# Eight very small loads ahead of the last but one store of a strided attention kernel

## Chip, cores and metric

The kernel runs on one core of a Trainium2 chip. The metric is the device time of one execution in microseconds (us); lower is better. Several runs of a kernel are given by their median.

## What is computed

Q, K and V are float32 arrays of 8 x 12 x 1024 x 64 (batch, head, position, depth). Every query attends to the 16 keys at the positions 0, 64, 128, ... of its head:

```python
attend_positions = np.arange(0, seq, stride)          # seq 1024, stride 64
k = K[:, :, attend_positions, :]
v = V[:, :, attend_positions, :]
scores = np.einsum('bhqd,bhkd->bhqk', q, k) * scale
weights = np.exp(scores - np.max(scores, axis=-1, keepdims=True))
weights = weights / (np.sum(weights, axis=-1, keepdims=True) + 1e-10)
result[:, :, i, :] = np.einsum('bhqk,bhkd->bhqd', weights, v)[:, :, 0, :]
```

All of Q is read (25.2 MB) and the whole output is written (25.2 MB); of K and V a sixteenth is read.

## The kernel before

The 96 heads are handled in NG = 24 groups of four. A group of Q is 1 MB and so is a group of the output. The work of a group runs through a pipeline whose steps are written out in the list ORDER: cast to bf16 (POOL, L352), transpose in 32x32 blocks (DVE, L368), scores (PE, L376), largest and subtraction (DVE, L398 and L402), exponential (ACT, L407), sums and reciprocals (DVE, L412 and L416), weights (POOL, L424), transposed weights (PE, L436, copied by ACT in L446), output products (PE, L452) and two copies of the output from PSUM to SBUF (ACT, L470). Q has 11 buffers (`qn`), the output 8 (`out_sb`, in four pairs).

`Program` records every operation with what it reads and writes; `plan` works out which waits are needed, and `emit` issues the operations engine by engine, with PE, DVE and ACT in loops for the middle groups. A transfer has a lane, which is a semaphore that it raises by 16 when it has landed.

All transfers are issued by SP, on one DMA queue, in this order: the rows of K (L288), group 0 of Q (the helper at L34), the rows of V into the tile `v_raw` (L288), groups 1 to 10 of Q, and then what `queue(g)` puts there as group g leaves the pipeline: the load of a later group into a buffer that has come free, and the store of the output. The stores of groups 0 to 15 are of 1 MB each; groups 16 to 21 go in three stores of 2 MB (two groups each); group 22 (`g == NG - 2`) has a store of its own. A store waits until ACT has copied the group (L470). `v_raw` is read by `values(...)` alone, on POOL (L336) and ACT, which spread V into `v_all` in the first microseconds of the kernel.

After the recorded operations SP waits for ACT's last one, a small copy at L579. POOL waits for all lanes whose name begins with `out` and frees the semaphores. SP goes through a few semaphore steps (L185), issues the store of group 23 (`end = send(NG - 1, 1)`, also at L34) and waits for it to land (L617). So the order on SP near the end is: store of groups 20 and 21, store of group 22, wait for ACT, store of group 23, wait for its landing.

Of the kernel before, what the change touches and what calls it, by code (L numbers as in the profile page):

```python
# [18 lines left out]
def _ap_with(ap: bass.AP, new_ap, extra_offset: int = 0) -> bass.AP:  # L19
    return dataclasses.replace(  # L20
        ap, ap=[list(p) for p in new_ap], offset=ap.offset + extra_offset
    )


def _copy(nc, out: bass.AP, in_: bass.AP):

    sides = [
        mybir.BassSymbolicTensorAccessPattern(
            ap=side.ap, dtype=side.dtype, bass_ap=side,
            is_dma=True, for_custom_bir_dma=True,  # L30
        )
        for side in (in_, out)
    ]
    return nc.sync.add_instruction(  # L34
        mybir.InstDMACopy(
            name=nc.get_next_instruction_name(), engine=mybir.EngineType.SP,
            ins=sides[:1], outs=sides[1:], queue="qSPDynamicHW",
            mode="Copy",
        )
    )  # L40


class Program:
# [9 lines left out]
    def op(self, engine, fn, reads=(), writes=(), after=(), lane=None, gate=None, gates=(), times=1, lands=None, last=False):  # L53
        i = len(self.ops)
        deps, own = set(after), set()
        for k in reads:
            deps.add(self.writer.get(k))
            own.add(self.writer.get(k))
        for k in writes:
            deps.update(self.readers.get(k, ()))  # L60
            deps.add(self.writer.get(k))
            own.add(self.writer.get(k))
        deps.discard(None)
        for k in reads:
            self.readers.setdefault(k, []).append(i)
        for k in writes:
            self.writer[k], self.readers[k] = i, []
        first, end, _ = self.loops.get(engine, (0, 0, 1))
        self.ops.append(dict(
            engine=engine, fn=fn, lane=lane or engine, deps=deps, own=own, gate=gate, gates=gates,  # L70
            times=times, lands=lands, last=last, looped=first <= self.turn < end,
        ))
        return i
# [142 lines left out]
def kernel(  # L216
# [8 lines left out]
    nc = tc.nc  # L225

    B, H, S, D = Q.shape
# [5 lines left out]
    NG = B * H // HG  # L233
# [19 lines left out]
    v_raw = sb.tile([P, NC, D], FP32, name="v_raw")  # L253
# [21 lines left out]
    op = prog.op  # L275
    stored = {}

    def load(g):
        n = 32
        op("SP", lambda: _copy(  # L280
            nc, qn[g % QBUFS],
            _ap_with(Q, [[HG * SD // n, n], [1, HG * SD // n]], g * HG * SD),
        ), writes=[f"qn{g % QBUFS}{h}" for h in range(2)], lane=f"q{g % QBUFS}")
# [10 lines left out]
    for g in range(1, QBUFS):  # L294
# [8 lines left out]
       writes=[f"k_t{c}{s}" for c in range(2) for s in range(4)])  # L303
# [183 lines left out]
    def store(g, n):  # L487
        both = range(g, g + n)
        sent = op("SP", lambda: send(g, n), lane=f"out{g % OBUFS}",
                  reads=[f"out{i % OBUFS}.{n}" for i in both for n in range(2)])  # L490
        stored.update((i, sent) for i in both)
# [38 lines left out]
    def queue(g):  # L530
        for n in range(g + QBUFS + ahead if g else QBUFS, g + QBUFS + ahead + 1):
            if n < NG:
                load(n)
        if g < SINGLE or g == NG - 2:
            store(g, 1)
        elif g % RUN == RUN - 1 and g < NG - 1:
            store(g - RUN + 1, RUN)

    def at(i, stage, lag):
# [28 lines left out]
        elif 0 <= g < NG and stage in stages:  # L568
            stages[stage](g)

    stages = dict(sums=sums, largest=largest, raise_=raise_, queue=queue)
    ORDER = "transpose0 turn3 spread3 sums2 cast-1 values2 outA4 largest1 evA4 outB4 evB4 scores0 weights2 raise_1 queue5".split()
    for i in range(2, NG + 5):
# [48 lines left out]
```

## Time and profile before

| | us |
|---|---|
| median of 3 runs | 129.3 (128.73, 129.30, 129.41) |
| the profiled execution | 129.4 |
| its span on the core | 127.6 |

| engine | busy us | share of the span |
|---|---|---|
| ACT | 95.1 | 75% |
| DVE | 86.4 | 68% |
| POOL | 76.5 | 60% |
| PE | 66.0 | 52% |

The span runs from the first to the last instruction of the program on the core; 1.8 us of the execution's time lie outside it. Times in the trace are us from the start of the span. In the rows of stretches each engine has its busy time and its count of instructions, and the last columns are the granted TensorE clock, the mean busy share of the core's 16 DMA engines, and GB/s; a packet counts in the stretch in which it starts, so that a share of a short stretch can be over 1. SPq stands for instructions that issue DMAs on SP, with the time that the issuing took; the time from the start of an issue to the landing of its data is given apart.

### The profile page before, as it was taken

Reading aid. Unit: us, or ns where it says so; the run is one execution under the profiler, and the core shown is the slowest. Engines: PE = TensorE matmul, PEld = TensorE weight load, DVE = VectorE, ACT = ScalarE, POOL = GpSimd, SP = SyncE. Lnnn points to the kernel's source line nnn. Section 1 sums busy time; section 2 is a strip of 40 time slices with the busy share of each in tenths; the row PEclk is TensorE's granted clock in tenths of the full one; section 3 lists DMA queues with packets and bytes.
Section 4 is the critical chain, followed back from the end, with each engine's and each line's share of the span. In section 5 each row is a group of like instructions: output and inputs, shape, how many; then the busy total and the mean of one; then the engine's idle time right before and its main releaser. Section 6 shows DMA issues by size and latency. Waiting matters only on the chain.

```text
span 127.6 us, 2563 instructions
## 1 busy us (share of the span) xinstructions
PE 66.0 (52%) x896; PEld 53.3 (42%) x896; DVE 86.4 (68%) x131; ACT 95.1 (75%) x118; POOL 76.5 (60%) x71
## 2 busy tenths in 40 slices
PE   0000896249666666666666666638446875940000
PEld 0000775148644445555555445426435763720000
DVE  4842597974999999999999999989559360000000
ACT  4259498119999999989999999895693999980000
POOL 2079959999688888888889887573765033000000
PEclk9999999855999999999999999995996899998555
DMA  2999999999979899899899999999899999999960
GB/s 52 408 390 390 483 411 421 462 390 452 442 336 526 339 424 501 357 416 478 377 437 444 401 439 470 385 449 475 357 413 437 419 437 431 426 442 416 401 280 18
DMA packets 7283, 51.15 MB, mean 401 GB/s; under 512 B 3824, under 2 KB 3824, under 8 KB 3824
## 3 DMA queue, kind: packets, MB, share of 16 engines
q1 hardware_dynamic: 7280, 51.12, 95.8%
q14 instruction: 3, 0.02, 0.1%
HBM read 25.95 MB, written 25.17 MB: 401 GB/s over the span
## 4 chain that ended last, share of the span: by engine, by line
DMA 21%; ACT 19%; DVE 16%; issue 6%; POOL 4%; PE 2%; SPq 0%; DVEq 0%; ACTq 0%
DMA qn<-in_Q_dram 21%; ACT out_sb L470 12%; DVE qt L368 6%; ACT wb L446 5%; DVE total L412 3%; DVE top L398 3%; ACT ex L407 2%; DVE low L402 2%; DVE rec L416 2%; PE tp L436 2%; POOL wt_all L424 2%; POOL qb L352 1%; POOL v_all L336 1%; PE o L452 0%; SPq L34 0%
## 5 line engine op out<-in xcount | busy, mean ns | idle before, releaser
L470 ACT COPY out_sb<-o 128x1024 f32<-128x1024 f32 x48 | 46.9, 1043 | 0.0
L352 POOL CAST qb<-qn 128x2048 bf16<-128x2048 f32 (+1 forms) x24 | 42.7, 1783 | 6.6 <-DMA qn<-in_Q_dram 6.4
L368 DVE STREAM_TRANSPOSE qt<-qb 128x1024 int32<-128x1024 int32 x24 | 29.8, 1241 | 9.4 <-POOL qb L352 9.3
L436 PE MATMUL tp<-identity,wt_all 128*128 128x128 bf16 x224 | 19.4, 236 | 31.4 <-POOL wt_all L424 30.1
L424 POOL TENSOR_TENSOR wt_all<-ex,rec 128x512 bf16<-128x512 f32 x24 | 25.4, 1057 | 16.5 <-DVE rec L416 16.3
L452 PE MATMUL o<-v_all,wb 128*128 x224 | 32.9, 294 | 1.4 <-ACT out_sb L470 1.4
L446 ACT COPY wb<-tp 128x1024 bf16<-128x1024 bf16 x25 | 25.6, 1025 | 8.6 <-PE tp L436 8.0
L376 PE MATMUL sc<-k_t,qt 128*128 x448 | 21.6, 201 | 15.4 <-DVE qt L368 14.5
L436 PEld LDWEIGHTS tp<-identity,wt_all 128*128 128x128 bf16 x224 | 14.4, 106 | 33.9 <-POOL wt_all L424 32.5
L376 PEld LDWEIGHTS sc<-k_t,qt 128*128 128x128 bf16 x448 | 18.3, 103 | 21.4 <-issue 20.1
L452 PEld LDWEIGHTS o<-v_all,wb 128*128 128x128 bf16 x224 | 22.3, 106 | 5.4 <-issue 1.3
L407 ACT ACTIVATE ex<-low 128x512 f32<-128x512 f32 x27 | 17.7, 655 | 4.8 <-DVE low L402 4.4
L412 DVE TENSOR_REDUCE total<-ex 128x32 f32<-128x512 f32 x24 | 15.6, 651 | 4.4 <-ACT ex L407 4.4
L402 DVE TENSOR_TENSOR low<-sc,top 128x512 f32<-128x512 f32 x24 | 16.6, 692 | 0.8
L398 DVE TENSOR_REDUCE top<-sc 128x32 f32<-128x512 f32 x24 | 15.2, 632 | 1.3 <-PE sc L376 1.3
L416 DVE RECIPROCAL rec<-total 128x32 f32<-128x32 f32 x24 | 8.5, 353 | 0.8
L309 POOL MEMSET v_all<- 128x4096 bf16 x1 | 3.5, 3511 | 5.2 <-DVE v_all L308 5.2
L336 POOL CAST v_all<-v_raw 32x128 bf16<-32x128 f32 (+1 forms) x12 | 5.1, 428 | 0.6
L322 ACT COPY k_t<-out_sb 32x384 bf16<-32x384 bf16 x8 | 4.1, 508 | 1.8 <-DVE out_sb L313 1.7
L349 ACT CAST qb<-qn 128x1024 bf16<-128x1024 f32 x3 | 3.1, 1040 | 0.0
L336 ACT CAST v_all<-v_raw 32x640 bf16<-32x640 f32 x4 | 2.9, 722 | 0.1
L302 DVE MEMSET k_t<- 128x1792 uint32 x1 | 1.6, 1552 | 1.9 <-issue 1.9
(17 smaller groups left out, 7.7 us busy)
## 6 DMA issues: line engine op xcount, KB each, us to landing
qn<-in_Q_dram SPq DMA_DIRECT2D x24, 1024.0 KB, 17.4
out_dram<-out_sb SPq DMA_DIRECT2D x18, 1024.0 KB, 19.0
out_dram<-out_sb SPq DMA_DIRECT2D x3, 2048.0 KB, 14.9
out_sb<-in_K_dram SPq DMA_DIRECT2D x1, 384.0 KB, 4.2
v_raw<-in_V_dram SPq DMA_DIRECT2D x1, 384.0 KB, 7.1
```

What stands on the lines that cost most here:

```text
L352: op("POOL", lambda: nc.gpsimd.tensor_copy(out=b[:, rows], in_=q[:, rows]), reads=[f"qn{g % QBUFS}{h}" for h in keys] + apart, writes=[f"q ...
L368: op("DVE", lambda *_: nc.vector.transpose(_ap_with(words, [words.ap[0], [1, 2], [D, 16], [2, 32]]), qb[g % 2].bitcast(I32),), reads=[f"qb ...
L376: r = nc.tensor.matmul(sc_ps[g % 2][:, 64 * i : 64 * i + 64], lhsT=_ap_with(qt[g % 2], [qt[g % 2].ap[0], [2, P]], extra_offset=2 * P * i + f),
L398: op("DVE", lambda *_: nc.vector.tensor_reduce(out=m, in_=s, op=ALU.max, axis=mybir.AxisListType.X,), reads=[f"sc{g % 2}"], writes=[f"top{ ...
L402: op("DVE", lambda *_: nc.vector.tensor_tensor(out=low, in0=s, in1=m.unsqueeze(2).to_broadcast([P, 32, NK]), op=ALU.subtract,), reads=[f"s ...
L407: op("ACT", lambda *_: nc.scalar.activation(out=ex[g % 2], in_=low, func=AF.Exp, bias=0.0, scale=scale,), reads=["low"], writes=[f"ex{g % ...
L412: op("DVE", lambda *_: nc.vector.tensor_reduce(out=total[g % 2], in_=ex[g % 2], op=ALU.add, axis=mybir.AxisListType.X,), reads=[f"ex{g % 2 ...
L424: op("POOL", lambda: nc.gpsimd.tensor_tensor(out=_ap_with(wt[g % 2], [wt[g % 2].ap[0], [32, 16], [4 * P + NK, 2], [1, NK]]), in0=ex[g % 2] ...
L436: r = nc.tensor.transpose(tp_ps[g % 2][:, 2 * c : 2 * c + 2, 64 * s : 64 * s + 64], wt[g % 2][:, s, c], identity,)
L446: op("ACT", lambda *_: nc.scalar.copy(wb[g % 2], tp_ps[g % 2]), reads=[f"tp{g % 2}"], writes=[f"wb{g % 2}"], gates=[("made", 3 * g + 7)])
L452: r = nc.tensor.matmul(_ap_with(o_ps, [o_ps.ap[0], [128, 2], [256, 2], [1, D]], extra_offset=512 * c + D * u,), lhsT=wb[g % 2][:, 2 * c + ...
L470: op("ACT", lambda *_: nc.scalar.copy(to[:, half], o_ps[:, half].rearrange("p c (b x) -> p c b x", b=2)), reads=[f"o{n}"], writes=[f"out{g ...
```

## The change

Just ahead of the store of group 22, SP issues eight loads from Q into the first rows of `v_raw`. The load number j (0 to 7) takes k rows of 4j + 4 float32 numbers, so 15 rows of 16 bytes, 14 of 32, 12 of 48, 8 of 64, 7 of 80, 4 of 96, 2 of 112 and 1 of 128: 63 rows with 3072 bytes in all. They have one lane, `outp`. Nothing reads what they bring. The first of them declares that it writes `v_raw`; the planner finds nothing that it has to wait for. Since the lane's name begins with `out`, POOL waits for it as for the stores before it frees the semaphores.

```diff
@@ -531,6 +531,11 @@
         for n in range(g + QBUFS + ahead if g else QBUFS, g + QBUFS + ahead + 1):
             if n < NG:
                 load(n)
+        if g == NG - 2:
+            for j, k in enumerate((15, 14, 12, 8, 7, 4, 2, 1)):
+                op("SP", lambda j=j, k=k: nc.sync.dma_start(
+                    v_raw[0:k, j, 0 : 4 * j + 4], _ap_with(Q, [[D, k], [1, 4 * j + 4]], j * 16 * D),
+                ), writes=["v_raw"] if not j else [], lane="outp")
         if g < SINGLE or g == NG - 2:
             store(g, 1)
         elif g % RUN == RUN - 1 and g < NG - 1:
```

## The prediction

> **What bounds the kernel now.** The first view is the page: the slices of DMA work, the queues and the issues.
>
> ```profile
> span 127.6 us, 2563 instructions
> ## 1 busy us (share of the span) xinstructions
> PE 66.0 (52%) x896; PEld 53.3 (42%) x896; DVE 86.4 (68%) x131; ACT 95.1 (75%) x118; POOL 76.5 (60%) x71
> ...
> DMA  2999999999979899899899999999899999999960
> GB/s 52 408 390 390 483 411 421 462 390 452 442 336 526 339 424 501 357 416 478 377 437 444 401 439 470 385 449 475 357 413 437 419 437 431 426 442 416 401 280 18
> ...
> q1 hardware_dynamic: 7280, 51.12, 95.8%
> ```
>
> The 16 DMA engines are nine tenths busy or more nearly all the time, on one queue; ACT, the busiest compute engine, has 75% of the span. The kernel moves 51 MB and is bound by that. So the question is what the change does to the transfers, and there to the end. The second view is SP's own waits in the last 20 us, the third SP's issues near the end, each in a window of its own, the fourth the stretches after the last compute.
>
> ```profile
> SPq L617 <- DMA out_dram<-out_sb: 11.4, 1, 11.4
> ...
> SPq L185 <- ACT edge L579: 1.9, 1, 1.9
> ```
> ```profile
> 108.60 0.54 SPq L34 DMA_DIRECT2D out_dram<-out_sb  x1
> ...
> 111.86 0.54 SPq L34 DMA_DIRECT2D out_dram<-out_sb  x1
> ...
> 114.84 0.54 SPq L34 DMA_DIRECT2D out_dram<-out_sb  x1
> ```
> ```profile
> L34 SPq DMA_DIRECT2D out_dram<-out_sb x1: 539/539/539, 114.8 to 114.8; - x1
> ...
> DMA to landing us min/median/max: 12.0/12.0/12.0
> ```
> ```profile
> 109.00:116.00 7.00, 3.92 (x53) 2.63 (x48) 0.00 (x0) 5.27 (x8) 0.00 (x0) 1.00 1.01 428
> ...
> 118.00:120.00 2.00, 0.00 (x0) 0.00 (x0) 0.00 (x0) 0.00 (x0) 0.00 (x0) 0.50 0.92 385
> 120.00:122.00 2.00, 0.00 (x0) 0.00 (x0) 0.00 (x0) 0.00 (x0) 0.00 (x0) 0.50 1.01 426
> 122.00:123.00 1.00, 0.00 (x0) 0.00 (x0) 0.00 (x0) 0.00 (x0) 0.00 (x0) 0.50 1.05 442
> 123.00:123.50 0.50, 0.00 (x0) 0.00 (x0) 0.00 (x0) 0.00 (x0) 0.00 (x0) 0.50 0.36 148
> 123.50:125.00 1.50, 0.00 (x0) 0.00 (x0) 0.00 (x0) 0.00 (x0) 0.00 (x0) 0.50 0.12 49
> 125.00:126.30 1.30, 0.00 (x0) 0.00 (x0) 0.00 (x0) 0.00 (x0) 0.00 (x0) 0.50 0.06 25
> 126.30:126.40 0.10, 0.00 (x0) 0.00 (x0) 0.00 (x0) 0.00 (x0) 0.00 (x0) 0.50 0.01 0
> ```
>
> SP issues its three last stores at 108.60 (groups 20 and 21), 111.86 (group 22) and 114.84 (group 23); then it waits 11.4 us for the last one, which lands 12.0 after its issue, at 126.8. The span ends 0.8 later. From 115 on nothing computes. What is left is a backlog: 385 to 442 GB/s, with the engines busy for 0.92 to 1.05, until 123. Then it tapers: a share of 0.12 (two engines of 16) up to 125, and 0.06 of 16, one single engine, up to 126.3. So the end is set by **one late DMA engine**, which finishes some 2.9 us after the bulk (126.3 less about 123.4). The other fourteen or so could be 2.9 us later at no cost.
>
> **What the change does, part by part.** It removes nothing and moves no instruction of PE, DVE, ACT or POOL. It adds eight DMAs to SP between the issues at 108.60 and 111.86, without a wait. There are two costs: SP's time to issue them, and the work of the DMA engines.
>
> *SP's time.* Eight issues of small transfers aren't in the trace. The nearest rows are the two loads of short rows (256 bytes, L288) and the large transfers:
>
> ```profile
> L288 SPq DMA_DIRECT2D out_sb<-in_K_dram x1: 435/435/435, 1.0 to 1.0; - x1
> L288 SPq DMA_DIRECT2D v_raw<-in_V_dram x1: 582/582/582, 2.2 to 2.2; - x1
> ```
> ```profile
> L34 SPq DMA_DIRECT2D qn<-in_Q_dram x24: 472/602/2046, 1.5 to 67.1; - x24
> ```
> ```profile
> 7.44 3.78 SPq L34 DMA_DIRECT2D qn<-in_Q_dram  x6
> ```
>
> The rows go from 0.44 to 2.05 us for one issue. Six issues in a row take 3.78 us, 0.63 each, with the gaps between them. For the small loads I take 0.6, between that and the two rows of L288 with such a gap. SP is free at 108.60 + 0.54 = 109.14; eight times 0.6 is 4.8, so the store of group 22 goes out at 113.9 to 114.0 in place of 111.86, 2.1 us late, and SP is through with it at 114.5. Queued behind it is SP's wait for ACT's last copy, and the last store:
>
> ```profile
> 113.96 0.32 ACT L579 COPY edge<-edge 128x1 f32<-128x1 f32 x1
> ```
>
> ACT is done at 114.28 and the last store follows 0.56 later, at 114.84. With SP free at 114.5 it would go out at 115.1, 0.2 late. Does anybody notice? The cover is the backlog. The bulk of the engines ends at about 123.4 and has the two last stores as its last work: each is 1.05 MB, at 426 GB/s 2.46 us, so that it begins on group 22 at about 123.4 - 4.9 = 118.5, and the late engine still later. From an issue to its first packet it takes 1.2 us at most, by the first load of all:
>
> ```profile
> 0.96 0.43 SPq L288 DMA_DIRECT2D out_sb<-in_K_dram  x1
> ```
> ```profile
> 0.00:1.90 1.90, 0.00 (x0) 0.00 (x0) 0.00 (x0) 0.57 (x1) 0.50 (x6) 1.00 0.00 0
> ...
> 2.10:2.20 0.10, 0.00 (x0) 0.00 (x0) 0.10 (x1) 0.10 (x1) 0.00 (x0) 1.00 0.50 138
> ```
>
> So the store of group 22 must be issued by 118.5 - 1.2 = 117.3. At 114.0 it is 3.3 us early, as it was 5.4 early before. The cost is **0**. If the cover were gone, it would be the whole 2.1. The cover ends where one issue takes over (117.3 - 109.14) / 8 = 1.02 us.
>
> *The DMA engines' work.* 3072 bytes are nothing at 426 GB/s; what counts is packets, and where they fall. The nearest row is the load of K, in a half microsecond that has only 256-byte packets:
>
> ```profile
> DMA packets 534, 0.14 MB, mean 273 GB/s; under 512 B 534, under 2 KB 534, under 8 KB 534
> ```
>
> It is the window from 3.1 to 3.6, and 16 engines x 500 ns / 534 = 15 ns for a packet. With 63 rows, 63 data packets and at most as many packets that raise the semaphore come to 126 x 15 = 1.9 us of engine time, 0.12 on each of the 16 engines. On fourteen of them it disappears in the 2.9 us that they are ahead; on the late one it counts in full, since that engine never idles until the end. If its share is none, it is 0; if it gets one row of each of the eight loads, 16 x 15 = 0.24. I take the mean, 63/16 = 3.9 rows, **0.12 us**.
>
> The Trainium skill, page "DMA: Bandwidth & Descriptors", section "Why a DMA increments its semaphore by 16 and not by 1", says that a DMA issued from SP runs on the largest number of engines up to 16 that divides its slowest dimension on both sides, and on the lowest-numbered of them. By that rule the loads run on 15, 14, 12, 8, 7, 4, 2 and 1 engines, engine 0 has all eight and engine 15 none. The same page, section "Latency and other measured facts", says that engines 7 and 15 are usually slower than the others, which would fit the two late engines here; they would have four rows or none, and the sum would have 0.12 or 0. No row of this trace carries an engine's number, so it doesn't show this.
>
> Loads between stores cost nothing by themselves. In the middle of the kernel they alternate one by one and the engines stay full:
>
> ```profile
> 36.00:64.00 28.00, 18.16 (x272) 14.39 (x271) 27.45 (x42) 27.58 (x35) 23.44 (x17) 1.00 1.00 425
> ```
>
> *POOL's wait.* The loads stand ahead of group 22's store in the queue, so they have landed before it; POOL waits for that store anyway, and nobody waits for POOL before the last landing at 126.8. Cost 0; it would be something only if a load landed after 126.8.
>
> *The sum.* 0 + 0.12 + 0 on the profiled execution's 129.4 (span 127.6 and 1.8 outside) gives 129.5. The median of the runs shown is 0.1 below that execution, so I predict **129.4**. The runs before spread from 128.73 to 129.41, so what can be told from no change is about 0.5%, 0.65 us. By itself this forecast reaches from 128.7 to 129.9.
>
> **The rivals.**
>
> *A. Slower: the completions of small loads queue up.* Each transfer ends with a write to a semaphore. The last store's data ends at 126.3 and it lands at 126.8, so such a write takes about 0.5 us. If an engine could have only one of these on the way, and the work behind it had to wait, eight in a row would cost each engine that carries them 0.5 each. On an engine of the bulk eight come to 4.0, 1.1 more than its 2.9 us of lead; on the late engine the mean of 3.9 comes to 2.0, and eight to 4.0. That gives 130.5 to 133.4, and with the mean 131.4. It decides from 2.9 / 8 = 0.36 us for one completion on the bulk, and from 0.65 / 3.9 = 0.17 on the late engine. For it: the kernel has no two completions close together in its full stretches, so the trace doesn't test it. Against it: a single completion stalls nobody. In the 28 us above some 11 transfers pass through each engine, one every 2.46 us; 0.5 lost on each would hold the share at 0.8, and it is 1.00. The same page of the skill, section "Anatomy of one DMA", gives a fixed cost of about 2.0 us to a DMA issued from GpSimd, most of it the receipt of the last write. An estimate by that figure, one after the other on the late engine, would be 3.9 x 2.0 = 8 us and 137; the 0.5 of this trace is far below it.
>
> *B. Slower: SP's issue becomes the bound.* If one issue takes 1.5 us, the store of group 22 goes out at 109.1 + 12 = 121.1, 3.8 after its latest moment; the bulk then ends at 127.2 in place of 123.4 and lands at 127.7, 0.9 after what it was, so 130.3. With the longest issue in the trace, 2.05, it goes out at 125.5, and 1.2 + 4.9 + 0.5 later, at 132.1, the end comes, 5.3 late, 134.7. For it is only that long row, which stands right behind the two loads of short rows; against it are the 0.44 and 0.58 of those loads themselves.
>
> *C. The change does not spread as it says.* If all 63 rows fall on one engine, that engine has 63 x 15 + 8 x 15 = 1.1 us more. On the bulk this is under its 2.9 us of lead, 129.4; on the late engine it is 130.5.
>
> *D. Faster.* The lag of the late engine is no fixed number: if the changed timing halved its 2.9 us, the end would come 1.4 earlier, at 128.0. Nothing in the change works that way, since it takes no byte from any engine; for it speaks only that the taper belongs to one engine.
>
> **How the numbers follow.** The forecast (all covered, up to 0.25 us on the late engine) has 0.66. A has 0.16, B 0.05, C 0.06, of which 0.02 slower, and D 0.07. So: within 0.5% 0.66 + 0.04 = 0.70, slower 0.16 + 0.05 + 0.02 = 0.23, faster 0.07. The range starts at 128.7, the lower end of the forecast, which leaves D out (0.07). Above, it goes on to A's low end, C's and B's with an issue of 1.5 us, and ends at 130.7; A's mean of 131.4 and what lies above is left out, about 0.13.
>
> **What the profile of the changed kernel would show.** Eight issues on SP between 109.1 and 114 with 0.4 to 0.6 us each, and the stores of groups 22 and 23 issued at about 114.0 and 115.1. The DMA share stays at 1.0 from 109 to 123, the taper still ends with a single engine, and the last landing comes within 0.3 of 126.8. A shows as a share well below 1.0 around 118 to 120, or as a longer taper; B as a hole over all engines before group 22's store; C as a longer single-engine tail with nothing else changed. The forecast is wrong if the taper gets longer by more than 0.65, or if the backlog at 109 is smaller than the bytes say.

## The result, and the profile after

| us | before | after |
|---|---|---|
| median of 15 runs each | 129.18 (128.69 to 129.43) | 129.76 (129.31 to 130.26) |
| the profiled execution | 129.4 | 129.58 |
| its span | 127.6 | 127.5 |

The ratio is 1.0046, with a 95% interval of 1.0028 to 1.0063: the changed kernel is slower by 0.6 us, 0.46%. That is at the border of what the prediction called no change. The spans of the two profiled executions differ by 0.1 us only; executions of one kernel differ by some tenths, so for sizes the means over all runs are used below. One execution of e9_split below, at 131.88 us, counts as slow and is left out of its row.

Each run has its time and its span. Their difference, the time outside the span, is 1.79 us on the average for the kernel before (23 runs of the first set of experiments) and 2.05 for the changed one (15 runs). The mean time of the 15 runs is 129.12 before and 129.71 after, so **0.26 of the 0.59 us lie outside the span and 0.33 in it**.

The page of the changed kernel, span and transfers:

```profile
span 127.5 us, 2571 instructions
...
DMA packets 7409, 51.15 MB, mean 401 GB/s; under 512 B 3950, under 2 KB 3950, under 8 KB 3950
...
q1 hardware_dynamic: 7406, 51.12, 96.0%
```

There are 126 packets more on the queue than the 7280 of before: 63 rows and 63 completions (writes to the semaphore). SP's issues near the end, from three windows, and the eight loads as a group (shortest, median and longest issue in ns):

```profile
108.24 0.54 SPq L34 DMA_DIRECT2D out_dram<-out_sb  x1
108.82 3.11 SPq L536 DMA_DIRECT2D v_raw<-in_Q_dram  x8
...
111.97 0.55 SPq L34 DMA_DIRECT2D out_dram<-out_sb  x1
...
114.48 0.55 SPq L34 DMA_DIRECT2D out_dram<-out_sb  x1
```
```profile
L536 SPq DMA_DIRECT2D v_raw<-in_Q_dram x8: 260/302/664, 108.8 to 111.7; - x8
```

The issues are shorter than expected, and the last two stores go out in good time. The last one lands 12.3 us after its issue, at 126.8, as before. The stretches of the end:

```profile
118.00:120.00 2.00, 0.00 (x0) 0.00 (x0) 0.00 (x0) 0.00 (x0) 0.00 (x0) 0.50 0.97 366
120.00:122.00 2.00, 0.00 (x0) 0.00 (x0) 0.00 (x0) 0.00 (x0) 0.00 (x0) 0.50 0.95 397
122.00:123.00 1.00, 0.00 (x0) 0.00 (x0) 0.00 (x0) 0.00 (x0) 0.00 (x0) 0.50 1.04 434
123.00:123.50 0.50, 0.00 (x0) 0.00 (x0) 0.00 (x0) 0.00 (x0) 0.00 (x0) 0.50 0.55 229
123.50:125.00 1.50, 0.00 (x0) 0.00 (x0) 0.00 (x0) 0.00 (x0) 0.00 (x0) 0.50 0.09 38
125.00:126.30 1.30, 0.00 (x0) 0.00 (x0) 0.00 (x0) 0.00 (x0) 0.00 (x0) 0.50 0.06 25
```

Between 118 and 122 the rate is some 25 GB/s lower than in the rows of before (385 and 426), and the bulk ends a little later; a single late engine still closes. The packets of the late engine can be read in one place. The window from 121.06 to 121.14, in slots of 2 ns:

```profile
DMA  0900920020029020020030020030002003020290
GB/s 0 4098 0 0 4096 2 0 0 8 0 0 2 4096 0 16 0 0 2 0 0 24 0 0 2 0 0 32 0 0 0 2 0 0 40 0 2 0 2 4096 0
DMA packets 17, 0.03 MB, mean 413 GB/s; under 512 B 13, under 2 KB 13, under 8 KB 13
```

A slot's rate times 2 ns is the size of the packet that starts in it: 2 is a semaphore's 4 bytes, 4096 a store's 8 KB, and 8, 16, 24, 32, 40 are the rows of 16, 32, 48, 64 and 80 bytes, about 13 ns apart with their completions. By then the bulk is past its small loads, so the late engine carries five of the eight, those of 15, 14, 12, 8 and 7 rows, in 0.06 us. The packets themselves are as cheap as forecast.

In the trace's records of single packets, the store packets that follow are 0.31 us long each, but on some half of the engines one of them, about 1.2 us behind the small loads, is stretched. On the late engine it takes 0.54 in place of 0.31; on the engines of the bulk the stretch grows with the small loads that an engine had, up to 0.5 us. So the late engine lost 0.06 + 0.23 = 0.29 us in this execution.

The records of landings show the completions themselves. On the late engine the store of groups 20 and 21 lands at 121.59, and the five small loads at 121.79, 121.99, 122.18, 122.38 and 122.57: **0.195 us apart**, where their packets were 13 ns apart and had all gone by at 121.13. The stretched packet ends at 122.90, 0.33 us after the last of these.

### The profile page after: what moved, and what is told of

Same layout as the page of the kernel before. It is cut to its first block, busy times and chain, and to the rows that moved or that the text cites. A ratio compares the mean times of both kernels' runs of the same rounds, so it can differ in the third digit from the quotient of the medians.

```text
span 127.5 us, 2571 instructions
## 1 busy us (share of the span) xinstructions
PE 64.3 (50%) x896; PEld 51.7 (41%) x896; DVE 86.4 (68%) x131; ACT 95.1 (75%) x118; POOL 76.4 (60%) x71
## 4 chain that ended last, share of the span: by engine, by line
DMA 21%; ACT 20%; DVE 16%; issue 6%; POOL 4%; PE 2%; SPq 0%; DVEq 0%; ACTq 0%
DMA qn<-in_Q_dram 21%; ACT out_sb L470 12%; DVE qt L368 6%; ACT wb L446 5%; DVE total L412 3%; DVE top L398 3%; ACT ex L407 3%; DVE low L402 2%; DVE rec L416 2%; PE tp L436 2%; POOL wt_all L424 2%; POOL qb L352 1%; POOL v_all L336 1%; PE o L452 0%; SPq L34 0%
## 5 line engine op out<-in xcount | busy, mean ns | idle before, releaser
L436 PE MATMUL tp<-identity,wt_all 128*128 128x128 bf16 x224 | 18.6, 230 | 32.6 <-POOL wt_all L424 31.3
L452 PE MATMUL o<-v_all,wb 128*128 x224 | 32.2, 290 | 1.4 <-ACT out_sb L470 1.4
L436 PEld LDWEIGHTS tp<-identity,wt_all 128*128 128x128 bf16 x224 | 13.7, 103 | 35.1 <-POOL wt_all L424 33.7
L452 PEld LDWEIGHTS o<-v_all,wb 128*128 128x128 bf16 x224 | 21.7, 104 | 5.2 <-issue 1.3
```

Of the source, the lines that this page charges most:

```text
L436: r = nc.tensor.transpose(tp_ps[g % 2][:, 2 * c : 2 * c + 2, 64 * s : 64 * s + 64], wt[g % 2][:, s, c], identity,)
L452: r = nc.tensor.matmul(_ap_with(o_ps, [o_ps.ap[0], [128, 2], [256, 2], [1, D]], extra_offset=512 * c + D * u,), lhsT=wb[g % 2][:, 2 * c + ...
```

## The experiments

The theories. **T** (later, with a number, S): each small load has a completion, and an engine works completions off one after the other; stores behind a row of them stall. It is the prediction's rival A with another price. **O**: the added time comes from outside the DMA engines. **P** and **V** divide the part outside the span: it comes with the number of SP's instructions, or with the different shapes of the loads. Each edit replaces the block of eight loads unless another place is shown. "In the span" is the mean span less the mean span of the runs of before beside it, "outside" the mean of time less span (1.78 to 1.79 for before). For the changed kernel the first is the mean time less what is outside, as above.

| kernel | ratio to before, 95% interval | in the span | outside |
|---|---|---|---|
| changed kernel | 1.0046 (1.0028 to 1.0063) | +0.33 | 2.05 |
| e1_four | 1.0042 (1.0020 to 1.0064) | +0.30 | 2.06 |
| e2_sixteen | 1.0108 (1.0083 to 1.0134) | +1.16 | 2.02 |
| e3_one | 1.0013 (0.9994 to 1.0031) | +0.18 | 1.78 |
| e4_many | 1.0380 (1.0354 to 1.0405) | +4.88 | 1.80 |
| e5_nops | 0.9994 (0.9985 to 1.0002) | -0.06 | 1.80 |
| e6_same | 1.0083 (1.0068 to 1.0098) | +0.95 | 2.02 |
| e7_spread | 1.0036 (1.0026 to 1.0046) | +0.20 | 2.06 |
| e8_lanes | 1.0094 (1.0077 to 1.0111) | +1.08 | 2.03 |
| e9_split | 1.0138 (1.0089 to 1.0186) | +1.41 | 2.07 |
| e10_sbuf | 1.0123 (1.0094 to 1.0151) | +1.37 | 2.05 |
| e11_mid | 1.0080 (1.0056 to 1.0104) | +0.87 | 2.04 |
| e12_single | 1.0021 (1.0003 to 1.0038) | +0.30 | 1.80 |

### e1_four: the loads on four engines

```diff
-            for j, k in enumerate((15, 14, 12, 8, 7, 4, 2, 1)):
+            for j, k in enumerate((4,) * 8):
```

> Eight loads of 4 rows each instead of 15 to 1: 32 rows, still eight issues on SP, eight transfers, the same semaphore and the same wait of POOL. Theory T (each small load costs the engines that carry it, the late one included, some 0.06 us, seen as one stretched store packet about 1.2 us after the loads): the loads fall on four engines, the late engine, which had five of the eight loads, has none, and the time is that of before, 129.2 (ratio 1.000 +- 0.002); four engines show the stretched packet. Rival O (the added time comes from outside the DMA engines: SP's eight issues, one more semaphore, POOL's longer wait): the time stays at 129.7 to 129.8 (ratio 1.0045).

The time did not fall back. Half of it is settled by the two columns: 0.27 of it is outside the span, where rival O has it. In the profiled execution four engines had the stretched packet, the late engine was not among them, and its last landing was at 126.7, as early as before. From the landing of the store of groups 20 and 21 to the last landing, the stretch in which the late engine meets the loads, it took 4.94 us in this trace, 4.94 in that of the kernel before and 5.16 in that of the changed kernel. But the mean span over 12 runs is 0.30 above that of before (standard errors of about 0.1). That is as much as the 0.33 of the changed kernel, so the means alone don't show that those 0.33 are the completions; the trace does, for one execution. Why the mean rose here is open: the late engine may be one of the four in some executions, which was not measured.

### e2_sixteen: the loads on all engines

```diff
-            for j, k in enumerate((15, 14, 12, 8, 7, 4, 2, 1)):
+            for j, k in enumerate((16,) * 8):
```

> Eight loads of 16 rows each: every engine, the late one included, has eight in place of five on the late one. Theory T: the late engine loses about 0.6 us (it lost 0.29 with five, and the engine with all eight had a stretched packet of 0.53), so some 0.3 more than the changed kernel, 130.0 (ratio 1.006 to 1.008), and all 16 engines show the stretched packet. Rival O: 129.7 to 129.8, as with the changed kernel (ratio 1.0045).

Theory T, and more than it said: 1.16 us in the span where 0.6 was expected, all 16 engines with the stretched packet, and the same 2.02 outside. Rival O alone falls. From the landing of the store of groups 20 and 21 to the last landing it took 5.71 us in this trace, and 5.71 to 5.74 in those of e6_same, e8_lanes and e10_sbuf below; in all seven traced kernels whose late engine meets no row of completions there (the kernel before, e1_four, e3_one, e5_nops, e7_spread, e11_mid, e12_single) it took 4.94. So 0.77 us of the 1.16 are placed; the rest is as open as the 0.30 of e1_four.

### e3_one: as many rows, one completion

```diff
+            op("SP", lambda: nc.sync.dma_start(
+                v_raw[:, 0, 0:16], _ap_with(Q, [[D, P], [1, 16]]),
+            ), writes=["v_raw"], lane="outp")
```

> One load of 128 rows of 64 bytes in place of eight loads: every engine has eight small data packets but one completion. Theory T in the form that completions cost: no stretched packet, 129.2 to 129.3 (ratio 1.000 to 1.001). Theory T in the form that the small data packets themselves cost: the stretched packet is there on all engines with about 0.5 us and the time is near 130.0 (ratio 1.006). Rival O: one issue in place of eight, 129.3 (ratio 1.000 to 1.002).

Eight small rows on each engine, as in e2_sixteen, but one completion: 0.18 in the span in place of 1.16, and no stretched packet. It is the completions that cost, not the rows. Outside the span nothing is added.

### e4_many: 24 completions

```diff
+            for j in range(24):
+                op("SP", lambda j=j: nc.sync.dma_start(
+                    v_raw[0:16, j % 12, 32 * (j // 12) : 32 * (j // 12) + 16],
+                    _ap_with(Q, [[D, 16], [1, 16]], j * 16 * D),
+                ), writes=["v_raw"] if not j else [], lane="outp")
```

> 24 loads of 16 rows of 64 bytes: every engine carries 24. Issues of 0.3 us take SP to about 116, still ahead of the moment at which the bulk of the engines needs the store of group 22 (117.3). Theory T: 24 times 0.06 to 0.08, so 1.5 to 1.9 us more on the late engine, 130.7 to 131.1 (ratio 1.012 to 1.015). Rival O, if its part grows with the count of issues: 0.55 x 3 = 1.7 us, about the same; if it is one semaphore or one wait, 129.7 to 129.8 (ratio 1.0045).

Far more than expected, 4.88 us, 0.2 for each load. But two things are mixed here. SP's issues, and the slice of GB/s near the end with the line of queues from the page:

```profile
108.95 11.33 SPq L536 DMA_DIRECT2D v_raw<-in_Q_dram  x24
120.34 0.55 SPq L34 DMA_DIRECT2D out_dram<-out_sb  x1
```
```profile
GB/s 53 392 437 457 348 467 477 397 397 477 457 315 422 514 362 407 531 338 420 514 380 385 506 429 355 487 447 345 424 424 419 457 417 422 437 338 91 350 199 15
...
q14 instruction: 4, 0.03, 0.1%
```

Loads of 16 rows take 0.47 us to issue with the gap between them, not 0.3, so the store of group 22 went out at 120.34, behind the 117.3 up to which the backlog covers it, and the bulk ran empty (91 GB/s in the 37th slice). That is the prediction's rival B, brought about. The late engine, though, came to its small loads only at about 121.5, so that its loss is mostly the 24 completions: from the landing of the store of groups 20 and 21 to the last one it took 9.36 us, 4.42 more than before, and the first store packet behind the 24 took 3.4 us by itself. Outside the span there is nothing, against theory P in its simplest form; note the fourth packet of the instruction queue, where all other pages have three.

### e5_nops: eight empty instructions

```diff
+            for j in range(8):
+                op("SP", lambda: nc.sync.nop())
```

> Eight empty instructions on SP in place of the eight loads; no transfer is added. In the runs so far the time outside the span is 2.02 to 2.06 us for the three kernels with eight loads of eight different row lengths and 1.78 to 1.80 for the kernel before and for the kernels with one load and with 24 equal loads. Theory P (the part outside the span comes with the number of SP's instructions, by where the program ends up): 2.05 outside, 129.3. Theory V (it comes with the different shapes of the transfers): 1.79 outside, 129.05. In the span nothing: 127.2 to 127.3 by both.

The program that ran has no empty instructions (its page counts 2563 instructions, as before), so this says nothing on P or V. It is a repeat of the kernel before, and shows how close two of the same come: 0.9994.

### e6_same: eight loads of one shape

```diff
+            for j in range(8):
+                op("SP", lambda j=j: nc.sync.dma_start(
+                    v_raw[0:16, j, 0:16], _ap_with(Q, [[D, 16], [1, 16]], j * 16 * D),
+                ), writes=["v_raw"] if not j else [], lane="outp")
```

> Eight loads of 16 rows of 64 bytes, all of one shape, in place of the eight row lengths of the 16-row experiment. Theory S (completions are worked off one by one on each engine, 0.2 us each, whatever the size): in the span the same as there, 128.4 on the average, 1.16 over before. Outside the span: theory P 2.05, so 130.4; theory V 1.79, so 130.2.

In the span as e2_sixteen within the scatter, so the size of the rows does not matter; outside 2.02, so V falls. How the completions hold the bulk is seen in three stretches of this kernel:

```profile
119.00:120.00 1.00, 0.00 (x0) 0.00 (x0) 0.00 (x0) 0.00 (x0) 0.00 (x0) 0.50 1.13 395
120.00:121.00 1.00, 0.00 (x0) 0.00 (x0) 0.00 (x0) 0.00 (x0) 0.00 (x0) 0.50 0.90 238
121.00:122.00 1.00, 0.00 (x0) 0.00 (x0) 0.00 (x0) 0.00 (x0) 0.00 (x0) 0.50 0.95 369
```

The engines count as busy (0.90), but fewer packets start: 238 GB/s, since each engine sits in one stretched packet. A share near 1 isn't a rate.

### e7_spread: the same eight loads, one at a time

```diff
+        if 8 <= g < 16:
+            op("SP", lambda: nc.sync.dma_start(
+                v_raw[0:16, g - 8, 0:16], _ap_with(Q, [[D, 16], [1, 16]], g * 16 * D),
+            ), writes=["v_raw"] if g == 8 else [], lane="outp")
```

> The same eight loads of 16 rows of 64 bytes, one ahead of each of the stores of groups 8 to 15 and none near the end. Theory S: a completion has 2.4 us until the next one, so none waits for another, and only the packets are left, 8 x 2 x 10 ns: the span is 127.3 to 127.5, the time 129.1 to 129.3 (with 0.26 more if theory P of the outside part holds). Rival (each completion costs the late engine some 0.15 wherever it stands, since that engine is never idle): 128.4 and 130.2, as in a train.

0.20 in the span, where eight in a row cost 0.95 on the same chip. The stretches of this kernel, over the loads and near the end:

```profile
68.00:104.00 36.00, 22.36 (x298) 18.30 (x299) 29.48 (x47) 30.84 (x38) 22.62 (x17) 0.91 1.02 428
119.00:120.00 1.00, 0.00 (x0) 0.00 (x0) 0.00 (x0) 0.00 (x0) 0.00 (x0) 0.50 1.01 426
120.00:121.00 1.00, 0.00 (x0) 0.00 (x0) 0.00 (x0) 0.00 (x0) 0.00 (x0) 0.50 1.07 451
```

428 GB/s with the loads in between: a completion with 2.4 us to itself stalls nothing. Outside the span are the same 2.06, with the loads nowhere near the end.

### e8_lanes: a semaphore for each load

```diff
-                ), writes=["v_raw"] if not j else [], lane="outp")
+                ), writes=["v_raw"] if not j else [], lane=f"outp{j}")
```
(against e6_same)

> As the experiment with eight equal loads in a row, but each load has a semaphore of its own, so that the trace gives the landing of each. Theory S: issued some 0.47 us apart, they land 0.195 apart, on the late engine from about 122.0 to 123.4, and the time is that of the equal loads. Rival (it is the common semaphore that holds them up, one address written by all): they land closer together than 0.1, the stretched store packets shrink, and the span falls back towards 127.4.

With a lane each, the trace gives every load's landing. The first and the last one:

```profile
109.25 0.60 SPq L536 DMA_DIRECT2D v_raw<-in_Q_dram  x1
...
112.71 0.42 SPq L536 DMA_DIRECT2D v_raw<-in_Q_dram  x1
```
```profile
DMA to landing us min/median/max: 13.1/13.1/13.1
...
DMA to landing us min/median/max: 11.0/11.0/11.0
```

They land at 109.25 + 13.1 = 122.35 and 112.71 + 11.0 = 123.7; a load lands with its slowest engine, which is the late one. The packets of all eight pass the late engine in about 0.1 us, but their completions arrive over 1.36 us, **0.195 us apart** (0.19 on the average of the other 15 engines, by the landing records). The common semaphore is not the cause. So the theory is now: on each engine one completion at a time, 0.2 us each or a little less; behind eight of them some four store packets (1.2 us) can be read, then the engine stalls; behind the 24 of e4_many the first packet already stalled. In the changed kernel the last of the late engine's five arrives 1.4 us behind its packet, since the completion of the store ahead of them takes the first 0.5; all but 0.23 was hidden.

### e9_split: taking work off the late engine

No small loads; the store of group 22 in pieces, meant to be faster.

```diff
+    def split(g):
+        for p, n in [(0, 96)] + [(p, 4) for p in range(96, P, 4)]:
+            op("SP", lambda p=p, n=n: part(g, p, n), lane=f"out{g % OBUFS}",
+               reads=[f"out{g % OBUFS}.{n}" for n in range(2)])
...
-        if g < SINGLE or g == NG - 2:
+        if g == NG - 2:
+            split(g)
+        elif g < SINGLE:
             store(g, 1)
```
(`part` issues the store of n partitions from partition p on)

> No small loads at all; the store of group 22 is cut in two kinds of pieces: one store of 96 partitions on all engines and eight of 4 partitions each, which run on four engines only. The late engine then has 6 packets of that store in place of 8, 0.61 us less, and the four engines have 14, 1.8 us more, within their 2.9 us of lead. If the late engine is not one of the four: the span falls by 0.6 to 126.8. If it is one of them, it rises by 1.8 to 129.2. Outside the span, theory P (eight more instructions on SP bring 0.26): 2.05, so 128.9 in all; without theory P 1.79 and 128.6.

It is slower by 1.4%. SP's issues and two stretches say where:

```profile
112.38 8.08 SPq L34 DMA_DIRECT2D out_dram<-out_sb  x8
...
121.29 0.60 SPq L34 DMA_DIRECT2D out_dram<-out_sb  x1
```
```profile
120.00:121.00 1.00, 0.00 (x0) 0.00 (x0) 0.00 (x0) 0.00 (x0) 0.00 (x0) 0.50 0.40 115
121.00:122.00 1.00, 0.00 (x0) 0.00 (x0) 0.00 (x0) 0.00 (x0) 0.00 (x0) 0.50 0.28 107
```

The eight small stores took SP 8.08 us, 1.0 each on the average (0.60 to 2.30), so the last store went out at 121.29 and most engines waited for it (115 and 107 GB/s). The late engine had six packets of that store as planned, and the stretch from the landing of the store of groups 20 and 21 to the last landing was shorter, 4.72 us in place of 4.94. But on it that earlier store landed at 122.5 in place of 121.9, and why is open. The traced execution, at 130.10 us, is one of the faster ones; the others in the row reach 131.50, and what they lost is not shown. For the other question it is clear: **2.07 outside, without a single small load**. It is the eight more issues on SP.

### e10_sbuf: no HBM in the loads

```diff
-                    v_raw[0:16, j, 0:16], _ap_with(Q, [[D, 16], [1, 16]], j * 16 * D),
+                    v_raw[0:16, j, 0:16], v_raw[32:48, j, 16:32],
```
(against e6_same)

> Eight copies from SBUF to SBUF, of 16 rows of 64 bytes, in place of eight equal loads from HBM. Theory S (the completions are the cost, one after the other): as with the equal loads, span 128.4, time 130.4. Rival (the small reads from HBM hold up what is behind them): the span falls back to 127.4 or so, the time to 129.5.

1.37 in the span, no less than with loads from HBM: the small reads from HBM are not what holds up.

### e11_mid: the same row of loads earlier

```diff
-        if g == NG - 2:
+        if g == 17:
```
(against e6_same)

> The eight equal loads of 16 rows in a row, ahead of the store of groups 16 and 17, some 30 us before the end, while SP waits long for ACT. Theory S with a late engine that never idles: a train costs the same anywhere, span 128.4, time 130.4 (ratio 1.0085). Rival (only near the end does it count, earlier the late engine catches up or all engines wait for each other): 127.5 and 129.5.

0.87: a row of completions costs nearly the same some 17 us earlier on the late engine, as it should if the late engine never catches up.

### e12_single: 16 loads on one engine

```diff
+            for j in range(16):
+                op("SP", lambda j=j: nc.sync.dma_start(
+                    v_raw[0:1, j % 12, 16 * (j // 12) : 16 * (j // 12) + 16],
+                    _ap_with(Q, [[D, 1], [1, 16]], j * 16 * D),
+                ), writes=["v_raw"] if not j else [], lane="outp")
```

> 16 loads of one row of 64 bytes each: all on a single engine, by the packets of the changed kernel not the late one; that engine then has 16 x 0.2 = 3.1 us of completions against 1.2 of run-ahead and 2.9 of lead, so nothing shows in the span: 127.4. If it were the late engine, the span would grow by 2.5 or more. Outside the span: one load more gave 1.78, eight 2.02 to 2.06, 24 gave 1.80; if the part comes in by where the last instructions fall, 16 can give either, and 2.05 or 1.79 alone would fit, no value between.

Outside the span it is 1.80, so 16 more instructions bring nothing there. But in the span are 0.30, and not by the late engine. The single engine takes its completions 0.18 us apart (by the landing records 16 of them from 118.85 to 121.57), within its lead. The last store's landing and the packets around the end (window 127.5 to 129) show where:

```profile
core 0 of [0], span 127.9 us
...
114.95 0.55 SPq L34 DMA_DIRECT2D out_dram<-out_sb  x1
```
```profile
DMA to landing us min/median/max: 11.9/11.9/11.9
```
```profile
DMA  0000000000000000008000000000000000000000
...
q14 instruction: 1, 0.01, 2.1%
```

The last landing is at 126.8 or 126.9, as before, but the span ends 1.1 later and not 0.8: SP loses some 0.3 us among its very last instructions. A packet of the instruction queue is recorded at 128.2, just behind the span. In e4_many, with 24 more instructions, the fourth packet of that queue is at 127.7, under the wait for the last store, and nothing is lost outside. With one more there is no sign of any of it. So a halt of about 0.3 us seems to move through the end of SP's program as instructions are put ahead of it: behind the span with eight more, in its last microsecond with 16, under the wait with 24. That its place goes with the count of SP's instructions is what the runs show; that it is a fetch of instructions is only argued from those two packets, and for eight no such packet is recorded.

## Why the prediction was right, and where it was not

The time lies in the range, and slower by 0.46% is within the 0.5% that was called no change. But the working had 0.12 us, and the change cost 0.59: it was luck that a band as wide as the scatter of the runs held two costs that the sum did not have.

- **What bounds the kernel**: right as far as it was tested. e2_sixteen and e12_single differ in whether the late engine carries completions: 1.16 us in the span against none besides the halt. The 0.30 of e1_four, whose late engine had none in the trace, does not fit in yet, and in e4_many and e9_split it was SP that left the bulk idle.
- **SP's time, cost 0**: right, with room. One issue took 0.26 to 0.66, with a median of 0.30, not 0.6. Behind another small load it goes with the rows: medians of 0.25 for one row, 0.30 for four, 0.42 for 16. It is no constant, though: the loads of e7_spread, one by one in the middle of the kernel, took 0.58 to 3.39, with a median of 1.59, as long as rival B had it. That the cover has an end is shown by e4_many and e9_split.
- **The DMA engines' work, 0.12**: this step was mis-sized. "16 engines x 500 ns / 534 = 15 ns for a packet" was right for packets (13 ns for a row with its completion on the late engine), but the completion costs 0.195 us of its own when another follows closely. In the one execution that was traced the late engine lost 0.29 us in place of 0.12. The mean span grew by 0.33, but with e1_four at 0.30 it is not settled how much of that is this.
- **Rival A** was the mechanism of what the late engine lost, with 0.195 in place of 0.5 and with 1.2 us that the engine can read ahead, which the rival did not have. The argument against it, "a single completion stalls nobody", was true and e7_spread shows it again; it could not speak against a row of eight, and the text said itself that the trace doesn't test it.
- **POOL's wait, cost 0**: nothing speaks against it; it was not tried alone.
- **"1.8 outside"** was carried over unchanged. It became 2.05, 0.26 us, nearly half of the whole, and no rival had it.
- **The Trainium skill's rule on the number of engines** ("DMA: Bandwidth & Descriptors", section "Why a DMA increments its semaphore by 16 and not by 1"): the trace agrees with its count, 63 completions for 15 + 14 + 12 + 8 + 7 + 4 + 2 + 1 engines. By its other half, the lowest-numbered engines, the late engine with just the first five loads is one of 4, 5 and 6. The same page's engines 7 and 15 ("Latency and other measured facts") would have had four or none, so they do not fit this execution; the page's guess at a reason is one for DMAs issued from GpSimd, and here SP issues all.
- **Rivals B, C and D** did not come in the changed kernel: SP was through with the store of group 22 at 112.5, and the rows spread over the engines. What B describes came in e4_many and e9_split; no run showed D.

Open are the 0.30 us in the span of e1_four, whether the late engine is the same one in each execution, and a kernel with less work on it that does not hold up SP.

## What to carry to other kernels

Count completions, not bytes: in a queue that is never empty, small transfers in a row cost an engine about 0.2 us each once its read-ahead is used up (four 8 KB packets behind eight of them, less behind 24), and the same transfers one by one between large ones, or as many rows in one transfer, cost about 0.2 us in all. Ask which engine ends last and whether it carries them; the others hide up to their lead. And for differences of a few tenths, compare the span and the time outside it apart, since a few instructions more on SP can bring 0.3 us at the end of the program that no transfer explains.

## What was not expected of the hardware

- Completions in a row on one DMA engine arrive 0.18 to 0.195 us apart (e12_single, e8_lanes), also with a semaphore for each; without HBM in the transfer they cost as much (e10_sbuf).
- A small store of 4 partitions took SP 1.0 us to issue on the average of a row of eight (e9_split); a small load from HBM took 0.25 to 0.42 behind another one near the end, and 1.59 alone in the middle of the kernel (medians; e7_spread for the last).
- Eight more instructions on SP brought 0.23 to 0.29 us outside the span in all nine kernels that had them, the changed one included; 1, 16 or 24 more brought none there.
